# Two of the head's seven transfers moved from the SyncE queue to ScalarE

## The chip, the cores and the metric

The kernel runs on one core of a Trainium2 chip. Times are microseconds of device time. "The time" of a kernel is the median of several executions; the profile and its trace are of one execution.

## The reference

One decoder layer, batch 1, 256 tokens, width 1024, float32. What is computed, cut to its core:

```
h = rms_norm(x, pre_mix_g);  u = h @ w_in                 # 1024 -> 2560 columns
y = concat(conformer_conv(u_conf), short_conv(u_sc), moba_attention(u_att), rglru(u_lru)) @ w_out
x = x + rms_norm(y, post_mix_g)
m = square(relu(rms_norm(x, pre_mlp_g) @ mlp_w1)) @ mlp_w2   # 1024 -> 4096 -> 1024
x = x + rms_norm(m, post_mlp_g)
```

## The kernel before

Activations are held transposed (128 rows of the width, 256 tokens); weights come from HBM as tiles of 128 x 2048 (1 MB). Most products are done in three passes over split numbers: ScalarE rounds a weight tile to a high part (`split_hi`, tiles `hi`), VectorE subtracts to get the low part (`split_lo`, tiles `lo`), and TensorE multiplies high by high, high by low and low by high.

The order of the work is written out by hand: each engine runs its instructions in the order of the text (the class `InOrder`, line 50). Waits between engines are semaphores that the framework places. It tells transfers apart by eight semaphores that are used in turn, so a transfer that comes ninth waits, before it is issued, for the one eight places ahead of it to land.

The start of the kernel, which the change touches, is the *head*: one DRAM tensor that holds the parameters, the transposed input in eight blocks `x0` to `x7` and eight blocks `w0` to `w7` (128 x 256 each) of the first columns of `w_in`. It is loaded into the tile `hd` by seven transfers on the SyncE queue (SP), in the order of `HEAD` (line 45):

```
HEAD = (("x0", "w0"), ("x1", "w1"), ("x2", "x3", "w2"), ("x4", "x5", "w3"), ("x6", "x7", "w4"), ("w5", "w6"), ("w7",))
```

The third to the fifth are 384 KB each, the sixth 256 KB, the seventh 128 KB. Behind them SP issues the first weight tiles (`load(1, 2)`, `load(2, 2)`, each in two halves, and `load(3)`, then `load(4)`), into tiles `raw_in`.

On these blocks the engines work as they come. VectorE scales each x block by its gain (`hf(k)`, tile `hF`), makes `ab` for a small parameter chain behind `hf(2)`, and adds up squares (`add`, tile `sq`). ScalarE loads the Exp table, then does `square(0)`, `h_hi(0)` (rounds to `hT`), `e` (an exponential of `ab`), `square(2)`, `square(4)`, `h_hi(2)`, `square(6)`, a table load for Sqrt, `h_hi(4)`, `h_hi(6)` and the first quarters of `split_hi(1)`. `square(k)` reads the blocks x_k and x_k+1. TensorE multiplies in float32, without splitting (`native(k)`, needs `hF` of block k and the block w_k): k = 0 to 6, then the sum of squares `pss`, then k = 7. From `pss` ScalarE and VectorE make `rstd`; TensorE spreads it as a row (`pR`), ScalarE copies that to `R1` (printed as `R`), and VectorE multiplies projections by it (`cg`, in `conf_gate` and `conf_val`). Behind that the projections of the four mixers follow, then the output projection and the MLP.

GpSimd, meanwhile, fills constants: `warm` for twelve TensorE warm-up products, `ident` (a 128 x 128 identity, a memset and an `affine_select`) and, after it has copied the parameters to `prm`, padding, `identb` (the identity in bfloat16, lines 278 and 279), `bones`, `dist` and others; later a chain of tiny operations that begins with a product of `sr` and `e`. `identb` is first used by `att_scores`.

Of the kernel before, what the change touches and what calls it, by code (L numbers as in the profile page):

```python
# [18 lines left out]
BF16 = mybir.dt.bfloat16  # L19
AF = mybir.ActivationFunctionType  # L20
# [4 lines left out]
P = 128  # L25
S = 256
# [16 lines left out]
PCOLS = C_MLP + KT  # L43

HEAD = (("x0", "w0"), ("x1", "w1"), ("x2", "x3", "w2"), ("x4", "x5", "w3"), ("x6", "x7", "w4"), ("w5", "w6"), ("w7",))
HOFF = {b: PCOLS + i * S for i, b in enumerate(sum(HEAD, ()))}
HCOLS = PCOLS + 2 * KT * S

# [17 lines left out]
def hybrid_layer(ctx, tc, x, head, win, wout, w1, w2, gates, rows, out):  # L66
    nc = tc.nc
    V, A, G, T, Q = (InOrder(tc, e) for e in (nc.vector, nc.scalar, nc.gpsimd, nc.tensor, nc.sync))

    cst = ctx.enter_context(tc.tile_pool(name="cst", bufs=1))  # L70
# [68 lines left out]
    hd = big.tile([P, HCOLS], F32, tag="yy", name="hd")  # L139
    xs = [cst.tile([P, D], F32, name=f"x{t}") for t in range(2)]  # L140
    gw = wk.tile([P, 4, P], F32, name="gw")
    c = 0
    for blocks in HEAD:
        n = HOFF[blocks[-1]] + S
        Q.dma_start(hd[:, c:n], head[:, c:n])
        c = n

    def hb(b):
        return hd[:, HOFF[b]:HOFF[b] + S]

    def xpair(k):
        a, b = HOFF[f"x{k}"], HOFF[f"x{k + 1}"] - HOFF[f"x{k}"]
        return hd[:, a:a + 2 * b].rearrange("p (k c) -> p k c", c=b)[:, :, :S]
# [13 lines left out]
    def pc(t, c, n=1):  # L167
# [8 lines left out]
    ident = cst.tile([P, P], F32, name="ident")  # L176
    G.memset(ident, 1.0)
    G.affine_select(out=ident, in_=ident, pattern=[[-1, P]], compare_op=ALU.is_equal, fill=0.0, base=0,
                    channel_multiplier=1)

# [22 lines left out]
    sr = wk.tile([P, 2], F32, name="sr")  # L206
    s2 = wk.tile([P, 2], F32, name="s2")
    q = wk.tile([P, 2], F32, name="q_")
    A.preload_act_table(AF.Exp)

    def hf(k):
        V.tensor_scalar(hF[:, k, :], hb(f"x{k}"), hd[:, C_PRE + k:C_PRE + k + 1], None, op0=ALU.mult)
# [62 lines left out]
    G.memset(xpad[:, :, :LK - 1], 0.0)  # L275
    cpad = wk.tile([P, 2, SK - 1 + S], F32, name="cpad")
    G.memset(cpad[:, :, :SK - 1], 0.0)
    identb = cst.tile([P, P], BF16, name="identb")
    G.tensor_copy(identb, ident)
    bones = cst.tile([P, P], F32, name="bones")  # L280
    G.memset(bones, 0.0)
    G.memset(bones[0:64, 0:64], 1.0 / 64)
# [962 lines left out]
```

## Time and profile before

| | us |
|---|---|
| median of 3 runs (lowest, highest) | 277.46 (276.95, 277.49) |
| the profiled execution, its own time | 277.3 |
| its span in the trace | 275.6 |
| TensorE busy (matmul) | 266.6, 97% |
| VectorE busy | 257.7, 93% |
| ScalarE busy | 187.9, 68% |
| GpSimd busy | 22.0, 8% |

The span runs from the first to the last instruction of the trace; the profiled execution's own time is 1.7 us longer. Busy shares are means over stages; which engine sets the time in a stage is read from the chain of work that ended last and from the waits. A timeline row gives start, duration, engine (PE is TensorE, PEld its weight loads, DVE VectorE, ACT ScalarE, POOL GpSimd, SPq SyncE's queue), operation, tiles, count, and in brackets the idle time before it with what ended it. All instructions show the one line L60, that of a helper, so the names of tiles tell them apart.

### The profile page before, as it was taken

To read this page: it belongs to the slowest core of one execution; us is meant where nothing else is said; L and a number is where in the kernel's file an instruction comes from. 1 tells how busy PE (TensorE), PEld (TensorE's weight loads), DVE (VectorE), ACT (ScalarE), POOL (GpSimd) and SP (SyncE) were. 2 spreads that over 40 slices of the span, in tenths; PEclk is the share of its full clock that TensorE was granted. 3 is DMA by queue.
4 is the path that set the end of the run, shared out by engine and by line. 5 is a ranking of instruction groups with operands and counts; after the bars stand their busy time and mean duration, and the time that the engine had idled before them with its cause. 6 is when DMAs were issued, how large, how long until landed. Compare 5 with 4: busy or idle time off the path is not lost.

```text
span 275.6 us, 4693 instructions
## 1 busy us (share of the span) xinstructions
PE 266.6 (97%) x1893; PEld 245.2 (89%) x1893; DVE 257.7 (93%) x350; ACT 187.9 (68%) x229; POOL 22.0 (8%) x53
## 2 busy tenths in 40 slices
PE   6999999999999999999999999999999999999991
PEld 4898997999987799899999999999999999999880
DVE  1989999999989999999999999999999999999874
ACT  3895669694557869868468777676885684777341
POOL 4388600000000000000000000000000000000000
PEclk9999999999999999999999999999999999999998
DMA  7998645938502825575375383473562653740004
GB/s 221 396 408 315 233 152 164 373 151 272 182 7 69 312 96 193 194 284 199 115 297 174 133 306 118 190 292 95 225 240 94 277 201 127 283 155 0 0 2 152
DMA packets 9237, 53.04 MB, mean 192 GB/s; under 512 B 1024, under 2 KB 1536, under 8 KB 3712
## 3 DMA queue, kind: packets, MB, share of 16 engines
q1 hardware_dynamic: 9216, 52.75, 51.7%
q8 instruction: 15, 0.25, 0.3%
q14 instruction: 6, 0.05, 0.0%
HBM read 51.70 MB, written 1.05 MB: 191 GB/s over the span
## 4 chain that ended last, share of the span: by engine, by line
PE 91%; DVE 3%; ACT 2%; DMA 2%; issue 1%; SPq 0%; DVEq 0%; ACTq 0%
PE pm L60 30%; PE m_acc L60 17%; PE pu L60 17%; PE acc L60 8%; PE m_sm L60 7%; PE m_mm L60 3%; PE pz L60 2%; DMA hd<-in_head_dram 2%; PE c L60 2%; DVE lo_in L60 1%; PE psc L60 1%; PE po L60 1%; ACT hi_in L60 1%; PE pg L60 1%; DVE u L60 1%
## 5 line engine op out<-in xcount | busy, mean ns | idle before, releaser
L60 DVE TENSOR_TENSOR lo_w<-raw_w,hi_w 128x2048 fp32r<-128x2048 f32 (+3 forms) x38 | 66.9, 1767 | 0.0
L60 ACT ACTIVATE hi_w<-raw_w 128x2048 fp32r<-128x2048 f32 (+2 forms) x35 | 54.5, 1600 | 1.3 <-issue 1.3
L60 ACT ACTIVATE th<-trs 128x2048 fp32r<-128x2048 f32 x13 | 24.9, 1916 | 13.0 <-DVE trs L60 13.0
L60 PE MATMUL pm<-h2T,hi_w 128*128 128x256 f32 x240 | 32.4, 278 | 0.0
L60 PE MATMUL pm<-h2T,lo_w 128*128 128x256 f32 x240 | 32.1, 276 | 0.0
L60 PE MATMUL pm<-h2L,hi_w 128*128 128x256 f32 x240 | 32.1, 276 | 0.0
L60 PEld LDWEIGHTS pm<-h2T,hi_w 128*128 128x128 f32 x240 | 29.9, 188 | 0.1
L60 DVE TENSOR_TENSOR tl<-trs,th 128x2048 fp32r<-128x2048 f32 x13 | 29.7, 2286 | 0.0
L60 PEld LDWEIGHTS pm<-h2T,lo_w 128*128 128x128 f32 x240 | 29.5, 188 | 0.0
L60 PEld LDWEIGHTS pm<-h2L,hi_w 128*128 128x128 f32 x240 | 29.5, 188 | 0.0
L60 DVE SCALAR_TENSOR_TENSOR cacc<-zpad,prm,cacc 128x256 f32<-128x256 f32 x60 | 25.4, 484 | 0.1
L60 ACT ACTIVATE mh<-mf 128x896 fp32r<-128x896 f32 (+2 forms) x16 | 14.1, 881 | 15.2 <-DVE mf L60 15.2
L60 PE MATMUL acc<-hi_out,yy 128*128 128x512 f32 x64 | 21.4, 402 | 0.0
L60 DVE TENSOR_TENSOR lo_in<-raw_in,hi_in 128x2048 fp32r<-128x2048 f32 (+1 forms) x11 | 20.9, 1900 | 0.2
L60 ACT ACTIVATE mr<-pm 128x512 f32<-128x512 f32 x15 | 8.9, 593 | 15.9 <-PE pm L60 15.9
L60 DVE TENSOR_TENSOR trs<-raw_w,trs 128x512 f32<-128x512 f32 x26 | 18.0, 692 | 0.9
L60 PE MATMUL pu<-hT,hi_in 128*128 128x256 f32 x128 | 17.9, 282 | 0.6 <-DVE cg L60 0.6
L60 PE MATMUL m_acc<-hi_w,ml 128*128 128x512 f32 (+1 forms) x57 | 17.9, 389 | 0.0
L60 PE MATMUL m_acc<-hi_w,mh 128*128 128x512 f32 (+1 forms) x57 | 17.7, 385 | 0.0
L60 PE MATMUL m_acc<-lo_w,mh 128*128 128x512 f32 (+1 forms) x57 | 17.7, 385 | 0.0
L60 PE MATMUL pu<-hT,lo_in 128*128 128x256 f32 x128 | 17.4, 278 | 0.1
L60 ACT ACTIVATE hi_in<-raw_in 128x2048 fp32r<-128x2048 f32 (+2 forms) x12 | 17.4, 1479 | 0.0
(235 smaller groups left out, 567.0 us busy)
## 6 DMA issues: line engine op xcount, KB each, us to landing
raw_w<-in_w_dram SPq DMA_DIRECT2D x32, 1024.0 KB, 4.8
raw_in<-in_win_dram SPq DMA_DIRECT2D x7, 1024.0 KB, 5.0
raw_out<-in_wout_dram SPq DMA_DIRECT2D x4, 1024.0 KB, 5.1
raw_in<-in_win_dram SPq DMA_DIRECT2D x4, 512.0 KB, 8.2
hd<-in_head_dram SPq DMA_DIRECT2D x3, 384.0 KB, 5.5
x<-in_x_dram SPq DMA_DIRECT2D x2, 512.0 KB, 6.3
grow<-in_rows_dram SPq DMA_DIRECT2D x2, 512.0 KB, 6.4
hd<-in_head_dram SPq DMA_DIRECT2D x2, 256.0 KB, 4.7
```

The lines of the kernel that those rows point to most:

```text
L60: ins = f(*args, **kwargs)
```

## The change

The transfers that end in the blocks `w3` (the fourth: x4, x5, w3) and `w6` (the sixth: w5, w6) are no longer issued by SP. ScalarE issues them, one after the other. Ahead of them on ScalarE stand the load of the Exp table, which was ScalarE's first instruction already and is only moved up in the text, and the cast of the identity to `identb`, which GpSimd did before. The cast waits for GpSimd's `ident`; the transfers themselves wait for no data.

```diff
+HEAD_A = ("w3", "w6")
@@
     for blocks in HEAD:
         n = HOFF[blocks[-1]] + S
-        Q.dma_start(hd[:, c:n], head[:, c:n])
+        if blocks[-1] not in HEAD_A:
+            Q.dma_start(hd[:, c:n], head[:, c:n])
         c = n
@@ (behind the affine_select of ident)
+    A.preload_act_table(AF.Exp)
+    identb = cst.tile([P, P], BF16, name="identb")
+    A.activation(identb, ident, AF.Copy)
+    for blocks in HEAD:
+        if blocks[-1] in HEAD_A:
+            A.dma_start(hd[:, HOFF[blocks[0]]:HOFF[blocks[-1]] + S], head[:, HOFF[blocks[0]]:HOFF[blocks[-1]] + S])
@@
-    A.preload_act_table(AF.Exp)
@@
-    identb = cst.tile([P, P], BF16, name="identb")
-    G.tensor_copy(identb, ident)
```

## Rows read from the trace of the kernel before

**Rows 1.** Chain of work that ended last, 0 to 30 us: start, us, what

```profile
1.71 4.80 DMA hd<-in_head_dram
...
6.94 4.66 PE pu L60 x20
...
14.09 0.39 ACT R L60
...
25.04 5.04 PE pu L60 x42
```

**Rows 2.** Busy time in stretches: stretch and length; per engine busy us (instructions); PEclk, DMA share, GB/s

```profile
25.00:260.00 235.00, 234.91 (x1693) 217.79 (x1694) 230.37 (x297) 165.01 (x192) 6.73 (x9) 1.00 0.50 186
13.00:25.00 12.00, 11.33 (x98) 10.93 (x96) 10.95 (x15) 9.92 (x12) 10.55 (x19) 1.00 0.94 369
```

**Rows 3.** Timeline of SP's queue: third to sixth head transfer, weights, eleventh issue

```profile
1.71 0.42 SPq L60 DMA_DIRECT2D hd<-in_head_dram  x1
2.17 0.43 SPq L60 DMA_DIRECT2D hd<-in_head_dram  x1
2.65 0.43 SPq L60 DMA_DIRECT2D hd<-in_head_dram  x1
3.12 0.44 SPq L60 DMA_DIRECT2D hd<-in_head_dram  x1
4.08 12.96 SPq L60 DMA_DIRECT2D raw_in<-in_win_dram  x7
6.52 0.33 SPq L60 DMA_DIRECT2D raw_in<-in_win_dram  x1
```

**Rows 4.** DMA issues, third to sixth head transfer: KB each, us from issue to landing

```profile
hd<-in_head_dram SPq DMA_DIRECT2D x1, 384.0 KB, 4.8
...
hd<-in_head_dram SPq DMA_DIRECT2D x1, 384.0 KB, 5.5
...
hd<-in_head_dram SPq DMA_DIRECT2D x1, 384.0 KB, 6.0
...
hd<-in_head_dram SPq DMA_DIRECT2D x1, 256.0 KB, 6.2
```

**Rows 5.** Busy time in stretches of the head (PE, PEld, DVE, ACT, POOL, as rows 2)

```profile
1.50:2.00 0.50, 0.50 (x5) 0.31 (x4) 0.00 (x0) 0.50 (x1) 0.22 (x1) 1.00 0.53 69
...
0.80:3.80 3.00, 2.64 (x12) 1.64 (x12) 0.00 (x0) 1.28 (x1) 0.85 (x6) 1.00 0.62 196
3.50:4.00 0.50, 0.40 (x2) 0.00 (x0) 0.17 (x1) 0.00 (x0) 0.14 (x1) 1.00 1.07 418
4.50:6.50 2.00, 1.83 (x8) 1.27 (x8) 0.44 (x2) 1.16 (x2) 1.60 (x10) 1.00 0.96 257
...
7.00:13.00 6.00, 6.00 (x31) 5.16 (x32) 5.35 (x15) 5.97 (x11) 1.42 (x4) 1.00 1.03 391
```

**Rows 6.** Timeline of ScalarE in the head

```profile
0.79 1.28 ACT L60 ACT_TABLE_LOAD   x1 [0.79 <-PEq L1237]
4.54 0.63 ACT L60 ACTIVATE sq<-hd 128x512 f32<-128x512 f32 x1 [2.46 <-DMA hd<-in_head_dram]
...
6.99 0.20 ACT L60 ACTIVATE e<-ab 128x2 f32<-128x2 f32 x1 [1.29 <-DVE ab L60]
...
8.75 0.61 ACT L60 ACTIVATE sq<-hd 128x512 f32<-128x512 f32 x1
```

**Rows 7.** Timeline of all engines, 0 to 18 us

```profile
4.24 0.29 POOL L60 CAST identb<-ident 128x128 bf16<-128x128 f32 x1
...
7.70 0.35 DVE L60 TENSOR_SCALAR hF<-hd 128x256 f32<-128x256 f32 x1 [0.48 <-DMA hd<-in_head_dram]
...
8.74 2.46 PEld L60 LDWEIGHTS pu<-hF,hd 128*128 128x128 f32 x12 [0.21 <-DVE sq L60]
...
11.34 0.49 POOL L60 TENSOR_TENSOR sr<-sr,e 128x2 f32<-128x2 f32 x1 [4.83 <-ACT hT L60]
```

**Rows 8.** Waits of SP's own queue, 0 to 20 us: us in total, times, longest

```profile
SPq L60 <- DMA hd<-in_head_dram: 2.4, 4, 0.8
```

## The prediction

> **What bounds the kernel now.** I read the chain of work that ended last first, because it says which stage a saving must come from. It starts with the third transfer of the head (issued at 1.71 us, on the chain for 4.80 us), goes through 20 native matmuls (6.94 to 11.60), then ScalarE's copy of the row of factors (14.09) and reaches the long stretch of TensorE work at 25.04 [rows 1]. Behind 25 us TensorE is simply full: 234.91 of 235 us up to 260 [rows 2]. So an edit of the head can move the end only by moving that 25.04; in between (13 to 25 us) TensorE is busy 11.33 of 12 us [rows 2], and the little slack there sits in a chain from ScalarE to VectorE that moves as a whole. The profiled execution is 277.3 us with a span of 275.6 us, so 1.7 us lie outside the span and I leave them alone; the median of the three runs, 277.46, lies 0.16 above it.
>
> Next the transfers. The head's seven transfers are handed in by SP about 0.46 us apart (1.71, 2.17, 2.65, 3.12 for the third to the sixth) but land 4.8, 5.5, 6.0 and 6.2 us after their issue, that is at 6.5, 7.7, 8.65 and 9.3 [rows 3, 4]. The time from issue to landing grows from transfer to transfer: they are not waiting to be issued, they are waiting for each other. The stretches say the same. From 3.5 us on the 16 DMA engines are busy for their whole time and move 418 GB/s, from 7 to 13 us 391 GB/s; only from 4.5 to 6.5 us do they move less, 257 GB/s, and there too they are busy (0.96) [rows 5].
>
> Last the engines behind them. ScalarE does a table load from 0.79 to 2.07 and is then idle until 4.54; from 6.99, when the third transfer has landed and VectorE has made `ab`, it works without a hole to 13 us (5.97 of 6.00 us) [rows 5, 6]. That is what matters: in ScalarE's chain only the third transfer is waited for. The fourth and the fifth arrive just in time for an engine that is already loaded.
>
> **The change, part by part.** Five head transfers stay on SP (first, second, third, fifth, seventh), two go to ScalarE (fourth 384 KB, sixth 256 KB), behind the cast of the identity; the cast leaves GpSimd.
>
> The cast. On GpSimd it takes 0.29 us at 4.24, and GpSimd later idles 4.83 us ahead of the product at 11.34 [rows 7]: removing it there is worth 0. On ScalarE this trace has no cast of 128x128; I bound it by GpSimd's 0.29 us for the same cast [rows 7] and by ScalarE's own 0.63 us for 128x512 [rows 6], and take 0.3, since it has a quarter of those columns. It stands behind the table load, which ends at 2.07, and needs the identity, which GpSimd makes ahead of its work on the head. Then two issues at SP's price, 0.42 to 0.44 us each [rows 3]; ScalarE's issuing is not in this trace, so from 0 to twice that. ScalarE is through at 2.07 + 0.3 + 0.9 = 3.3 us (at worst 2.07 + 0.63 + 1.8 = 4.5), and its first work on the head starts at 4.54 [rows 6]. Cost 0; the cover is that idle stretch, and without it the price would be these 1.2 us. Queued behind them on ScalarE is the first `square`, which waits for the second transfer anyway.
>
> SP's queue. The fifth transfer moves up from 2.65 to 2.17, the seventh to 2.65, and the first weight loads from 4.08 to about 3.1 [rows 3]. What that is worth: the DMA engines are not out of work from 3.5 us on [rows 5], so an earlier place in a queue brings no byte earlier, unless another transfer gives way. The weights win nothing either: the list of waits up to 25 us has no engine that waits for `raw_in`. Worth 0. The Trainium skill says this as a rule (DMA: Bandwidth & Descriptors, section "Issuing engines are not separate DMA queues"): issuing from several engines saves only the sequencer's time, usually small against the transfer. The trace agrees: 0.44 us of issue against 6.2 us to the landing. By a sum that credited issue time instead, 0.9 us would be saved.
>
> The order of arrival. Here is the cost. From 0.8 to 3.8 us the engines move 196 GB/s, 588 kB [rows 5], which is just the first and the second transfer (by the code 618 and 512 columns of 128 x 4 bytes, 579 kB); so the third begins to move at about 3.8 us in the mean. In before everything stands in one queue, and the fourth cannot pass the third. In the change the fourth is handed in between 2.07 and 2.7 us, in another queue. The first transfer, issued at 0.8, moves its first bytes between 1.5 and 2.0 us [rows 5], about 1 us after its issue, so the fourth is ready at 3.1 to 3.7 us, when the third has hardly begun. The engines are full, so each byte of the fourth moved before the third is complete is a byte by which the third is late. The whole fourth is 393 kB; at 418 to 391 GB/s that is 0.94 to 1.01 us. The sixth follows it in ScalarE's queue at once, 262 kB, 0.63 to 0.67 us. No row of before shows two queues of loads side by side, so the delay of the third is bounded by 0 (strictly by time of issue) and by 0.98 + 0.65 = 1.63 us (both of ScalarE's transfers ahead of it). If both queues are served alike, the fourth is through when the third is (same size), and if that starts while the second still moves, the fourth ends early and part of the sixth gets in too. I take the fourth and half of the sixth: 0.98 + 0.32 = 1.3 us, so the third lands at 7.8 us. The Trainium skill describes that service in the same page, section "Queues, rings and completion order": each DMA engine takes turns between the queues that have work. That no run here shows; by it alone the third would be 1.0 to 1.6 us late.
>
> What follows from that. VectorE's `hF` for x2 and `ab`, then ScalarE's `e` at 6.99, all wait for the third, and move to 8.3. Behind `e` ScalarE's chain has no hole, so it is 1.3 us late as a whole. The fourth is then there before it is wanted: VectorE's wait of 0.48 us at 7.70 and TensorE's 0.21 us at 8.74 [rows 7] vanish, but they are not what ends last. The fifth lands behind the sixth, at 8.65 + 0.65 = 9.3 us; `square` on x6, now at 8.75 [rows 6], is due at 10.05, so that hides. The delay therefore goes to the copy at 14.09, to 25.04 and to the end.
>
> Sum: 277.3 + 1.3 + 0 (cast) + 0 (issues) + 0 (SP) = 278.6 us against the profiled execution, 278.76 against the median; I say 278.7. With a delay between 0.65 us (what the sixth alone is worth) and 1.63 us the forecast's own range is 278.1 to 279.1.
>
> **The rivals.** (a) Served in order of issue. Two queues make no difference if the engines take the work as it was handed in; the fourth, handed in at 2.1 to 2.7, then stands beside the fifth, where it stood. For: nothing in the trace speaks against it. Against: the two wait in different queues and something must choose. Gain: TensorE's 0.21 us at most, since ScalarE has no hole to give; 277.1 to 277.5 us.
>
> (b) Faster: the slow spell is cured. From 4.5 to 6.5 us the engines move 257 GB/s instead of 418, so 514 kB take 2.0 us that would take 1.23 [rows 5]. If the engines are held up there because one queue leaves them waiting, a second queue fills the gaps and the third lands up to 0.77 us earlier, with all of the chain: 277.46 - 0.77 = 276.7 us. This decides if the rate in that stretch comes near 400 and the third is not passed. Against: the engines count as busy there (0.96) [rows 5], so the packets themselves are long.
>
> (c) The issues wait. SP itself does not run free: it waits four times, 2.4 us in all, for head transfers to land; its eleventh issue goes at 6.52, when the third has landed [rows 3, 8]. If ScalarE's transfers are counted as they stand in the text, behind ten of SP's, the fourth is the eleventh, leaves at 6.5 and, at the third's 4.8 us, lands at 11.3 instead of 7.7: 3.6 us late for `square` on x4, about 281 us. Against: SP hands in its eighth transfer only at 4.08 [rows 3], long after ScalarE is ready, so by time both stand among the first eight.
>
> **How the numbers follow.** Forecast 0.70, (a) 0.12, (b) 0.12, (c) 0.06. Predicted 278.7 us. The range runs from 277.1, the lower end of (a), to 279.4, the forecast's upper end with 0.3 for a fifth transfer that is late as well; outside lie (b) and (c), 0.18. A measurement of this kernel tells 0.2%, 0.55 us, from no change: faster (under 276.9) 0.12, that is (b); within, (a) and 0.03 of the forecast for a delay under its range, 0.15; slower, the rest of the forecast and (c), 0.73.
>
> **What would show it.** Right: the third transfer lands at 7.5 to 8.1 us instead of 6.5; the fourth lands with it or before; ScalarE's `e` is at 8 or later; TensorE's gap near 25 us sits 1 to 1.6 us later; behind it nothing changes. ScalarE's two issues lie between 2.1 and 3.4 us. Wrong: the third lands at 6.5 as now (a), or before with 400 GB/s from 4.5 to 6.5 us (b), or ScalarE's issues stand behind a wait for a landing (c). I am also wrong if the delay shrinks between 8 and 25 us, which needs slack that I did not see.

## The result, and the profile after

| | before | after |
|---|---|---|
| median, us (lowest, highest), 11 runs each | 277.15 (276.64, 277.74) | 279.72 (278.96, 282.08) |
| ratio, 95% interval | | 1.009 (1.007 to 1.0109) |
| the profiled execution, its own time | 277.3 | 279.05 |
| its span in the trace | 275.6 | 277.3 |

The change makes the kernel slower, by 2.57 us on the medians. A second comparison (e7_after, below) gives 279.34 against 277.42, 1.92 us, ratio 1.0061 (1.0047 to 1.0075). The two profiled executions differ by 1.75 us, and these the traces can account for.

The chain of work that ended last, of after, 0 to 30 us (start, us, what), against [rows 1]:

```profile
1.69 6.16 DMA hd<-in_head_dram
...
11.25 1.97 PE pu L62 x8
...
13.56 1.91 PE pu L62 x12
15.72 0.38 ACT R L62
...
26.67 3.35 PE pu L62 x27
```

The third transfer takes 6.16 us instead of 4.80, and the copy `R` is at 15.72 instead of 14.09. The long stretch of TensorE's work begins at 26.67 instead of 25.04: 1.63 of the 1.75 us are lost before that point. Its beginning follows the row `pu x12` by 13.11 us here (26.67 - 13.56), and by 13.1 to 13.3 us in every kernel of this study, and from that row to the end of the span it is 263.6 to 264.1 us in all of them. So the start of `pu x12` (13.56 here, 11.94 in before) will stand for a kernel's loss in the head.

ScalarE's queue, VectorE and TensorE in the timeline of after, against [rows 3, 6, 7]:

```profile
1.75 0.38 ACTq L62 DMA_DIRECT2D hd<-in_head_dram  x1
2.08 0.31 ACT L62 ACTIVATE identb<-ident 128x128 bf16<-128x128 f32 x1
...
4.45 0.34 ACTq L62 DMA_DIRECT2D hd<-in_head_dram  x1
...
4.83 0.63 ACT L62 ACTIVATE sq<-hd 128x512 f32<-128x512 f32 x1 [2.44 <-DMA hd<-in_head_dram]
...
7.88 0.35 DVE L62 TENSOR_SCALAR hF<-hd 128x256 f32<-128x256 f32 x1 [2.94 <-DMA hd<-in_head_dram]
...
8.29 4.93 PE L62 MATMUL pu<-hF,hd 128*128 128x256 f32 x20 [1.38 <-DVE hF L62]
...
8.34 0.20 ACT L62 ACTIVATE e<-ab 128x2 f32<-128x2 f32 x1 [2.35 <-DVE ab L62]
```

Two things differ from what the prediction assumed. The fourth transfer is handed in at 1.75 us, 0.06 us behind the third and ahead of the cast, while the table load (0.79 to 2.07, as in [rows 6]) still runs. The sixth is handed in only at 4.45 us, just when the second transfer has landed (4.43): in the compiled program each transfer, whichever engine issues it, takes the next of eight completion semaphores. By the semaphore numbers in the trace the fourth is the eighth in that order, and the sixth the tenth: it gets the one of the second transfer, and its issue waits until that is given back.

The landings in after, third, fourth and sixth transfer (KB, us from issue to landing), against [rows 4]:

```profile
hd<-in_head_dram SPq DMA_DIRECT2D x1, 384.0 KB, 6.2
...
hd<-in_head_dram ACTq DMA_DIRECT2D x1, 384.0 KB, 6.3
...
hd<-in_head_dram ACTq DMA_DIRECT2D x1, 256.0 KB, 6.7
```

To the hundredth, by the trace's semaphore records, the third is there at 7.85 us instead of 6.50, the fourth at 8.03 instead of 7.67, the sixth at 11.12 instead of 9.35. The sum of the profiled loss closes with two terms. The 20 native matmuls begin at 8.29 instead of 6.94, 1.35 us later, behind the third. And they take 4.93 instead of 4.66 us, 0.27 us more: the last 8, which need the sixth, begin at 11.25, 0.13 us behind its landing, as in e6_late6 and e7_after (0.14 and 0.13). The chain above names VectorE there, whose last `hF` ends at 11.18, because of two waits it takes the one that ended last; but the first of these matmuls needs `hF` of x5, done at 10.05. The two terms together are 1.62 of the 1.63 us.

Busy time in stretches of after (columns as in [rows 2]), against [rows 5, 2]:

```profile
4.50:6.50 2.00, 2.00 (x7) 1.72 (x8) 0.44 (x2) 1.15 (x2) 1.44 (x8) 1.00 0.99 373
6.50:8.50 2.00, 0.62 (x3) 0.22 (x3) 0.62 (x4) 0.17 (x2) 0.00 (x0) 1.00 0.99 332
7.00:13.00 6.00, 4.60 (x20) 3.79 (x21) 4.86 (x15) 4.63 (x9) 0.49 (x1) 1.00 1.01 378
```

From 4.5 to 6.5 us the DMA engines move 373 GB/s where they moved 257, and still the third is late. ScalarE is busy for 4.63 us between 7 and 13 us instead of 5.97, and from 6.5 to 8.5 us all engines stand almost still.

What the rate doesn't show, the shares do. Each head transfer is split into sixteen shares, and in the trace's records its completion semaphore is raised sixteen times, once as each share arrives; the last one is the landing. The shares of the third transfer, with the sixth's landing, the marker, and the time at which the trace's records of TensorE's granted clock begin (of which the last section tells), in the trace of every kernel (us):

```
kernel            third's shares    the other    sixth    pu x12   clock
                  together, by      shares at    lands    at       recorded from
before            15, 5.43          6.50          9.35    11.94    4.18
e1_before         14, 5.43          6.41, 6.43    9.63    12.18    6.59
e4_cast           15, 5.39          6.24          9.30    11.87    5.40
e6_late6          15, 5.41          6.15         11.07    13.51    6.89
e8_fourth_later   15, 5.44          6.95          9.35    12.80    7.18
e11_both_later    13, 5.42          6.07, 6.60,   9.95    13.15    4.58
                                    7.79
e3_sixth          14, 5.90          6.87, 7.96    8.17    13.31    4.10
after             15, 6.16          7.85         11.12    13.56    5.59
e7_after          15, 6.24          8.12         11.46    13.90    5.78
e10_nowait2       14, 6.13          7.67, 7.85   10.46    13.57    6.02
e2_fourth         16, 6.26                        8.22    13.07    8.51
e5_nowait         16, 6.12                        8.25    12.39    7.19
e9_second         16, 5.59                        9.24    13.21    8.15
```

In before the last share of the third comes 1.07 us behind the other fifteen: that one share is the wait at the head of the chain [rows 1]. In after the fifteen come 0.73 us later than in before, and the last one 1.69 us behind them.

### The profile page after: what moved, and what is told of

Same layout as the page of the kernel before. It is cut to its first block, busy times and chain, and to the rows that moved or that the text cites. A ratio compares the mean times of both kernels' runs of the same rounds, so it can differ in the third digit from the quotient of the medians.

```text
span 277.3 us, 4690 instructions
## 1 busy us (share of the span) xinstructions
PE 267.7 (97%) x1893; PEld 246.2 (89%) x1893; DVE 257.6 (93%) x350; ACT 188.0 (68%) x230; POOL 21.5 (8%) x52
## 3 DMA queue, kind: packets, MB, share of 16 engines
HBM read 51.70 MB, written 1.05 MB: 190 GB/s over the span
## 4 chain that ended last, share of the span: by engine, by line
PE 89%; DVE 4%; DMA 2%; ACT 2%; issue 1%; SPq 0%; DVEq 0%; ACTq 0%
PE pm L62 30%; PE m_acc L62 17%; PE pu L62 15%; PE acc L62 8%; PE m_sm L62 7%; PE m_mm L62 3%; DMA hd<-in_head_dram 2%; PE pz L62 2%; PE c L62 2%; DVE lo_in L62 1%; PE psc L62 1%; PE po L62 1%; ACT hi_in L62 1%; PE pg L62 1%; DVE u L62 1%
## 5 line engine op out<-in xcount | busy, mean ns | idle before, releaser
L62 PE MATMUL pu<-hL,hi_in 128*128 128x256 f32 x128 | 17.5, 279 | 0.0
```

Source lines behind the costliest of these rows:

```text
L62: ins = f(*args, **kwargs)
```

## The experiments

Except where an edit says otherwise, each kernel has the cast and the table load as in the change, and only the set of transfers that ScalarE issues differs.

**The kernel before, again** (no edit).

> The kernel before once more, as a second trace and for the granted clock of each of its executions. All theories: third head transfer lands near 6.5 us, ScalarE's e starts near 7.0, 277.2 us. Theory 'order of arrival' (T1): the slow spell of the DMA engines between 4.5 and 6.5 us (257 GB/s) is there again or not, it is not what the change is about. Theory 'clock' (T3: the part of the loss that the profiled execution doesn't show is TensorE's granted clock falling in a longer hole of the head): every execution of this kernel has a clock of 0.996 or more.

Measured: 277.52 us against 277.62, ratio 0.9993 (0.9984 to 1.0003). The third lands at 6.4 us and `pu x12` is at 12.18. From 4.5 to 6.5 us the engines moved 221 GB/s, so the slow spell of [rows 5] is no accident of one trace. What theory 3 expected did not come: the mean granted clock of the twelve executions runs from 0.993 to 0.998, not from 0.996 up.

**The changed kernel, again** (no edit to it).

> The changed kernel again, for a second trace and a paired time. If its loss is a matter of order, the third transfer lands at 7.5 to 8.0 us, ScalarE's second issue goes out at about 4.4 us, the sixth transfer lands near 11 us, and the median is 2.0 to 2.6 us above the kernel before. If the landing of the third is a matter of chance (one DMA engine that straggles in some executions), it may land near 6.2 us here, with the sixth still near 11 us and the native product of x5 still waiting for it.

Measured: 279.34 us against 277.42, ratio 1.0061 (1.0047 to 1.0075). Chain of e7_after, 0 to 30 us:

```profile
4.54 6.92 DMA hd<-in_head_dram
11.59 1.97 PE pu L62 x8
13.90 1.91 PE pu L62 x12
```

The third landed at 8.1 us, the sixth was again handed in with the second's landing (4.54) and was there at 11.46; here the chain itself goes through it. Both are as in after, and a little later; the median is 1.92 us above the kernel before, just under the 2.0 to 2.6 expected.

**The cast alone.**

```diff
-HEAD_A = ("w3", "w6")
+HEAD_A = ()
```

> Only the cast and the table load stand as in the change (the cast on ScalarE ahead of its first square, the table load asked for earlier in the program, GpSimd's cast gone); all seven transfers stay on SyncE's queue, and no weight tile is written first. Theory 1 (all of the change's loss is in the transfers): the third lands near 6.5 us, e starts near 7.0 and the median is within 0.2 us of the kernel before. Theory 2 (the earlier cast itself costs time, which would be in every kernel of this study but the one before): the median is 0.5 to 1.2 us above the kernel before.

Measured: 277.69 us against 277.56, ratio 1.0009 (0.999 to 1.0028). Chain of e4_cast, 0 to 30 us:

```profile
4.30 7.22 PE pu L62 x28
11.87 1.89 PE pu L62 x12
...
24.96 5.04 PE pu L62 x42
```

The head ends 0.07 us earlier than in before. Theory 1 holds: the cast and the earlier table load cost nothing that can be measured, so the whole loss is in the two transfers.

**The sixth alone, with its wait.**

```diff
-HEAD_A = ("w3", "w6")
+HEAD_A = ("w6",)
```

> Only the sixth transfer (w5, w6) is issued by ScalarE; the other six stay on SyncE's queue, and the first weight tile is loaded as before. ScalarE's issue is expected to wait for the landing of a transfer of the head and to be handed in after 3.5 us instead of 2.9. Theory 1 (in the changed kernel the time is lost because the sixth transfer is handed in late and the native product of x5 waits for it): the third transfer lands near 6.5 us as in the kernel before, the sixth lands between 9.5 and 11 us, the matmuls of w5 and w6 are late by what it lands later than 9.6, and the median is 0.5 to 1.5 us above the kernel before. Theory 2 (the time is lost because a second queue beside the third transfer holds that one up): nothing moves beside the third here, so e starts near 7.0 us and the median is within 0.3 us of the kernel before.

Measured: 279.32 us against 277.42, ratio 1.0056 (1.0042 to 1.0071): as slow as the changed kernel beside it (279.34). Timeline of e6_late6:

```profile
3.81 0.38 ACTq L62 DMA_DIRECT2D hd<-in_head_dram  x1
...
6.18 0.35 DVE L62 TENSOR_SCALAR hF<-hd 128x256 f32<-128x256 f32 x1 [1.22 <-DMA hd<-in_head_dram]
...
6.63 0.20 ACT L62 ACTIVATE e<-ab 128x2 f32<-128x2 f32 x1 [1.01 <-DVE ab L62]
...
11.21 1.97 PE L62 MATMUL pu<-hF,hd 128*128 128x256 f32 x8 [1.05 <-DMA hd<-in_head_dram]
```

ScalarE's issue goes out at 3.81 us, with the first transfer's landing, and the sixth lands 7.26 us later. The third is on time (6.15 us) and `e` is even 0.36 us earlier than in before, and yet TensorE stands still for 1.05 us until the sixth is there at 11.07. Theory 1 holds, and costs more than the 1.5 us that it allowed. The late sixth by itself is enough for the whole loss.

**The sixth alone, at once.** So that its issue needs no landing, ScalarE writes one column of the first weight tile ahead of that tile's load, which overwrites it; the load then stands behind ScalarE's issue in the order of the semaphores. The kernels e2, e5, e8, e10 and e11 do the same. No kernel has that write alone; it takes 0.19 to 0.20 us between 2.3 and 2.9 us, where ScalarE is idle otherwise.

```diff
+HEAD_A = ("w6",)
@@
-    load(1, 2)
-    load(2, 2)
-    load(3)
@@ (behind ScalarE's issues)
+    w_, d_ = new_raw(1)
+    A.activation(w_[:, :1], ident[:, :1], AF.Copy)
+    for i in range(2):
+        Q.dma_start(w_[:, part(i, 2)], d_[:, part(i, 2)])
+    load(2, 2)
+    load(3)
```

> Only the sixth transfer (256 KB) on ScalarE behind the cast, again without a wait for a landing (the same one-column write). T1: it is handed in at about 1.75 us, beside the third, and moves beside it: third late by 262 kB at 400 GB/s, 0.65 us, lands at 7.1 to 7.2; the sixth lands before 8; 277.7 to 278.0 us. T2: third at 6.5, 277.2 us or a little less.

Measured: 278.82 us against 277.62, ratio 1.005 (1.0031 to 1.007). Chain of e3_sixth:

```profile
1.71 6.25 DMA hd<-in_head_dram
...
8.39 4.58 PE pu L62 x20
13.31 1.91 PE pu L62 x12
```

This is the other half of the loss by itself. The sixth, handed in at 1.75 us, is there at 8.17, before it is needed; the third, beside it, lands at 7.96 instead of 6.50, and the 20 matmuls run behind it without a hole (4.58 us) but begin 1.45 us late. By bytes 262 kB should have cost some 0.65 us: theory 1 had the direction, and missed the landing (7.1 to 7.2) and the time (277.7 to 278.0).

**The fourth alone, at once.**

```diff
+HEAD_A = ("w3",)
```

> Only the fourth transfer (384 KB) on ScalarE behind the cast; a one-column write of ScalarE into the first weight tile keeps SP's weight loads behind it in the count of transfers, so that ScalarE's issue waits for no landing. T1 (third is late by what of ScalarE's queue moves beside it, and the sixth's wait for a landing is a second, smaller loss): third lands at 7.5 to 7.9 us, e at 8.0 to 8.4, the sixth on SP lands by 9.6 and TensorE has no hole before native 5; 278.2 to 278.6 us. T2 (the late sixth is the loss, two queues cost nothing by themselves): third at 6.5, 277.2 us. T3: as T1 in the profile, but with single executions 1 to 3 us longer at a clock under 0.995.

Measured: 278.15 us against 277.62, ratio 1.0029 (1.0011 to 1.0046), single runs from 277.43 to 279.99. In the profiled execution (278.54) all sixteen shares of the third came together and it landed at 6.26, earlier than in before, not at 7.5 to 7.9 as theory 1 had it, and still `pu x12` was at 13.07. There the matmuls themselves were slow: see the last section. So this trace does not show what the fourth costs the third; theory 2, no cost, does not hold either, since the median lies 0.53 us above before. Nor does theory 3: the executions of 279.24 to 279.99 us have a clock of 0.997 to 0.998.

**Both at once, without the wait**, two kernels with the same text.

```diff
 HEAD_A = ("w3", "w6")
```

> The changed kernel with both transfers on ScalarE, but without the sixth's wait for the landing of the second (the same one-column write). T1: sixth issued at about 2.2 us and landed by 9.6, TensorE's hole of 0.48 us before native 5 gone; third at 7.8 to 8.4, since part of the sixth now moves beside it too; 278.5 to 279.2 us, a few tenths under the changed kernel. T2: the whole loss is gone, 277.2 us. T3: executions scatter as in the changed kernel (279 to 282) with clocks down to 0.987.

> Both transfers on ScalarE, handed in at 1.75 and 2.2 us with no wait for a landing (the first weight tile is written in one column first, which its load overwrites), once more, for a second trace. Its execution shown so far had the third land at 6.15 us, with no DMA engine behind the others, and was quicker than most of its runs. Theory 1 (a DMA engine that is behind the others in most executions takes packets of both queues in turn, and so holds up the third when the fourth moves beside it): here the third lands at 7.3 to 8.0 us, e starts near 8.2, TensorE's gap near 25 us starts at 26.0 or later, and the sixth lands by 9 us. Theory 2 (the third is always early in this kernel and the loss lies behind it): the third lands by 6.4 us again and the time is lost in the matmuls of the fourth to seventh transfer.

Measured: 278.71 us against 277.62, ratio 1.0045 (1.0029 to 1.0062), and 279.19 against 277.56, ratio 1.0054 (1.0037 to 1.0071). Landings of the third and the fourth, first in e5_nowait, then in e10_nowait2 (KB, us from issue to landing):

```profile
hd<-in_head_dram SPq DMA_DIRECT2D x1, 384.0 KB, 4.4
hd<-in_head_dram ACTq DMA_DIRECT2D x1, 384.0 KB, 4.9
```

```profile
hd<-in_head_dram SPq DMA_DIRECT2D x1, 384.0 KB, 6.2
hd<-in_head_dram ACTq DMA_DIRECT2D x1, 384.0 KB, 6.8
```

One text, handed in at the same times, and the third lands at 6.12 in one execution and at 7.85 in the other. In the first no share is behind the others, in the second two are. So theory 1 of the first expectation missed the third (7.8 to 8.4) in its trace and had the sixth (8.25) and the median right, and theory 1 of the second holds for the third. It was wrong on the sixth: handed in at 2.17 us it landed at 10.46, fourteen of its shares came by 8.51 and the last two at 9.54 and 10.46, and the fifth in SP's queue was held up with it (10.26). Chain of e10_nowait2:

```profile
8.28 1.99 PE pu L62 x8
10.40 2.83 PE pu L62 x12
13.57 1.91 PE pu L62 x12
```

With the sixth's wait gone, TensorE waits for the fifth instead, and `pu x12` is where it is in after. On the medians the wait's removal brings 0.3 to 1.5 us (1.63 and 1.1 us above before, against 1.92 and 2.57), and the intervals overlap in part: it helps, at most, a part of the way.

**The fourth alone, later.** An operation that reads the cast's result stands ahead of the issue.

```diff
+HEAD_A = ("w3",)
+    A.activation(w_[:, :1], identb[:, :1], AF.Copy)
@@ (then the issue)
```

> Only the fourth transfer (x4, x5, w3) is issued by ScalarE, and behind an operation that reads the cast's result, so it is handed in at about 2.5 us instead of 1.75, when the third (handed in at 1.7) has begun and the fifth (2.2) is in its queue. The first weight tile has one column written first, which its load overwrites. Theory 1 (transfers of two queues move roughly in the order in which they are handed in): the third is ahead of it and lands at 5.5 to 6.6 us, the fourth moves beside the fifth and lands at 8 to 9 us, and the median is 0 to 0.8 us above the kernel before. Theory 2 (two queues take turns whenever both hold something): the fourth moves beside the third from its start, the third lands at 7.3 us or later, e starts at 7.8 or later, and the median is 1 us or more above.

Measured: 278.61 us against 277.42, ratio 1.0038 (1.0023 to 1.0054). The issue went out at 2.44 us, fifteen shares of the third came by 5.44 as in before, and it landed at 6.95; the fourth landed at 8.63 and TensorE had waited for it (chain: the transfer from 2.44 for 6.19 us, then matmuls at 8.77), `pu x12` at 12.80. Neither theory fits whole: the third lies between their landings, and the time, 1.19 us above before, is theory 2's by way of the fourth, which is late in its turn (8.63 against 7.67).

**Both later.**

```diff
 HEAD_A = ("w3", "w6")
+    A.activation(w_[:, :1], identb[:, :1], AF.Copy)
@@ (then the two issues)
```

> Both transfers on ScalarE, behind an operation that reads the cast's result and with no wait for a landing: handed in at about 2.45 and 2.85 us, when the third (1.7) is ahead of them. The first weight tile is written in one column first, which its load overwrites. Theory 1 (a transfer moves in the order of its handing in, over both queues): the third lands at 6.2 to 7.0 us, the fourth at 8.3 to 8.9, the sixth at 9 to 10, and the median is 0.8 to 1.3 us above the kernel before, as with the fourth alone (278.6 there), so 0.5 us or more below the changed kernel. Theory 2 (two queues take turns whenever both hold something): the third lands at 7.3 or later and the median is 1.3 us or more above the kernel before.

Measured: 278.69 us against 277.56, ratio 1.0037 (1.0023 to 1.005). Chain of e11_both_later:

```profile
1.69 6.10 DMA hd<-in_head_dram
...
8.23 4.58 PE pu L62 x20
13.15 1.89 PE pu L62 x12
```

The median is where theory 1 put it, for a reason that is not theory 1's. Handed in 0.74 us behind the third, the fourth left thirteen shares of it alone (5.42 us, as in before), but the other three came at 6.07, 6.60 and 7.79, the last 2.37 us behind the thirteen, with two transfers in ScalarE's queue by then. The sixth, handed in at 2.85, landed at 9.95 and was on time: with the wait gone and the fifth in time too (9.54), the third's delay alone is left, and costs 13.15 - 11.94 = 1.21 us in the trace and 1.13 us on the medians.

**The second alone,** as ScalarE's first instruction, so that SP hands in each later transfer some 0.5 us earlier.

```diff
+HEAD_A = ("w1",)
@@ (the issue stands ahead of the table load)
```

> Only the second transfer (x1, w1) is issued by ScalarE, as its first instruction, ahead of the table load; so SyncE hands in each later transfer some 0.5 us earlier, the third at 1.2 us. The cast runs on ScalarE as in the change. If the issues of the head bind (one queue hands in 256 KB each 0.5 us), the third lands 0.3 to 0.5 us earlier than 6.5, e starts at 6.5 to 6.7 us and the median is 0.2 to 0.5 us below the kernel before. If the bytes bind, or the second and the third then move beside each other, the third lands at 6.5 or later and the median is within 0.3 us of the kernel before or above it.

Measured: 279.75 us against 277.42, ratio 1.0074 (1.0055 to 1.0092). In the profiled execution (278.7, the fastest of its six) the third did land early, at 5.59 us, but the first, which then has the second beside it, landed at 4.53 instead of 3.81. The 28 matmuls follow it without a hole, from 5.05 instead of 4.34 us: 0.71 of the 13.21 - 11.94 = 1.27 us there. The other 0.56 is in the matmuls, whose first ones were slow (last section). Neither branch of the expectation has this; what the other executions lose beyond it no trace shows. No kernel of the study is faster than before.

## Why the prediction was wrong in size and right in direction

**What bounds, right.** The loss is in the head, it passes 25 us unchanged, and the rest of the span is the same: 275.6 - 25.04 = 250.56 us behind the marker in before, 277.3 - 26.67 = 250.63 in after.

**The cast, SP's queue, the issues' own time: right, 0.** e4_cast shows it for the cast; the seventh's earlier issue and the weights' bring nothing that a trace shows, though no kernel has them alone.

**The third transfer, right in its landing, wrong in its terms.** Forecast 7.8 us and `e` at 8.3; measured 7.85 and 8.34. But the sum of bytes, 0.98 for the fourth and 0.32 for half of the sixth, is not what happened, so that the landing agrees is luck. The sixth had no part in it, being handed in at 4.45. Sharing the rate with the fourth cost fifteen of the shares 0.73 us, less than a whole fourth. The other 0.62 us is a last share that falls further behind. One to three shares are behind in ten of the thirteen traces: the last of them comes 0.7 to 1.1 us after the shares that came together where nothing of a second queue moves beside the third (before, e1, e4, e6), and 1.5 to 2.4 us after them where something does (e3, e8, e10, e11, after, e7). In e2 and e5 none is behind, with the fourth beside the third as in after. The reading that fits is one DMA engine that is behind and serves both queues: in after the last share of the fourth comes only 0.18 us behind that of the third, though the other fifteen of the fourth are through by 7.14. In after ScalarE's queue moves 66 packets of 3072 bytes from 5.0 to 6.0 us, and from 6.5 to 7.5 only two in each 0.5 us, as SP's fifth and seventh pass it. e3_sixth (the third at 7.96 with 262 kB beside it) and e11_both_later (7.79 with nothing beside thirteen of the shares) speak against the sum by bytes. That the share belongs to one DMA engine is an inference: the records give the count of shares, not which engine served them, and what holds it up was not found. Nor does one share of 24 KB explain the 257 GB/s of [rows 5], which is low for all engines together; that stays open as well.

**The sixth, the step that failed.** "The sixth follows it in ScalarE's queue at once" was wrong, and with it "The fifth lands behind the sixth": it came at 9.00, the sixth 2.1 us after it. Rival (c) had the mechanism, with a chance of 0.06 and for the wrong transfer: it let the fourth wait and argued that by time both stand among the first eight. The order that counts is that of the compiled program: the fourth is the eighth transfer there, the sixth the tenth. So the sixth was handed in at 4.45 us and landed at 11.12, where the forecast had no term at all. In the profiled execution that term is 0.27 us, because the third's delay covers the rest; alone it is 1.57 us (e6_late6: 13.51 - 11.94). The two losses lie side by side: 1.2 to 1.4 us for the third alone (e11_both_later, e3_sixth), 1.57 for the sixth alone, 1.62 for both. Both must go for the head to be as before; in e11_both_later the sixth's part went and 1.2 us stayed.

**The size.** The profile's 1.75 us against the forecast's 1.3 is 0.27 for the sixth, 0.05 for the third and 0.12 behind the head. The median's 2.57 us is more than any trace of after shows. Its profiled execution was the second fastest of eleven; the one of e7_after, 279.57, has the third at 8.12 and the sixth at 11.46, so `pu x12` is at 13.90, 1.96 us late. How far the last share falls behind differs from one execution to the next, and the range, whose upper end was a sum of bytes with 0.3 us on top, had no room for that. The two longest executions of after, 282.08 and 281.24 us, have the lowest mean granted clock of the eleven, 0.987 and 0.992, against 0.993 to 0.998; but in e2_fourth 279.99 us came at 0.997 and 277.67 at 0.993, and neither of the two has a trace. So what made them long stays open. Nor is it known what the other executions lose beyond the traces: a clock that rises late, as in e2_fourth (last section), would add to them, but no trace of them was kept.

**Rivals (a) and (b).** Something of (a) holds, only that the fourth, handed in at 1.75 instead of 2.1 to 2.7 us, stands beside the third and not the fifth. Its first packet moves at 3.91 us, when the second transfer, handed in at 1.22, is nearly through (last packet at 3.98). The sixth, though its queue was otherwise empty for fifteen shares, moved its first packet at 8.03 us, when fifteen shares of SP's fifth and seventh (handed in before it) were in, and then side by side with the first weight tile; in e6_late6, handed in at 3.81, at 7.61, when the first shares of the seventh arrive (7.50). In e11_both_later the fourth left thirteen of the third's shares alone. In these traces transfers handed in within 0.1 us of each other take turns, later ones mostly come later. The Trainium skill (DMA: Bandwidth & Descriptors, section "Queues, rings and completion order") lets each engine take turns between the queues that hold work for it. For the third and the fourth the trace of after agrees, with 118 packets of 3072 bytes from ScalarE's queue against 131 from SP's from 4 to 6 us. For the sixth, counted from its hand-in, it does not: the first packet came 3.6 us later; whether its work had reached the engines before, the records do not show. Of (b) the cure came, 373 GB/s for 257, and brought nothing, since the bytes that filled the spell were the fourth's and not the third's missing share. There was little to gain: in e1_before and e4_cast the third is not on the chain at all, TensorE's 28 matmuls run without a hole from the first transfer on (4.30 to 11.53 us in e4_cast).

## What to carry to other kernels

A transfer that is moved to another engine's queue takes its place in the order of the program's completion semaphores with it: count which transfer's landing its issue will have to wait for, and price the landing from there, not from when the engine is free. A transfer has landed when its last share has: before crediting or charging bandwidth, see whether all shares come together, and do not put another queue's transfer beside the one that the chain waits for. And where two transfers are made late at once, price each alone and take the larger, then see what each removal would leave.

## What the runs showed of the hardware that was not expected

ScalarE hands in a transfer while its table load runs (1.75 us, load from 0.79 to 2.07) and ahead of an operation that stands before it in the text (the cast, at 2.08): its place in the text does not hold it back. In e8_fourth_later an operation ahead of it that waits for the cast's result did, and it went out at 2.44.

The third transfer's last share comes 0.7 to 2.4 us behind the group in ten of the thirteen traces listed above; in three (e2_fourth, e5_nowait, e9_second) all sixteen come together. In e9_second it is the fourth whose last share is behind: fifteen by 6.86 us, its landing at 7.58.

The first native matmuls run at two rates, and the change from one to the other comes at another time in each execution, in before as well. TensorE's native matmuls between 5 and 5.5 us in the kernel before and in e1_before, and between 5.5 and 6 us in e2_fourth (duration in ns, min/median/max, then first and last start):

```profile
L60 PE MATMUL pu<-hF,hd x4: 379/379/379, 4.7 to 5.3; 128*128 128x256 f32 x4
```

```profile
L60 PE MATMUL pu<-hF,hd x3: 634/634/796, 4.3 to 5.3; 128*128 128x256 f32 x3
```

```profile
L62 PE MATMUL pu<-hF,hd x3: 634/634/634, 5.0 to 5.9; 128*128 128x256 f32 x3
```

Those of 634 ns follow each other by 0.43 us, those of 379 ns by 0.215: a factor of two, as between the clock's two levels, 1.2 and 2.4 GHz. The trace's records of the granted clock agree. They begin, with the full clock, at the times in the last column of the table, and in all thirteen traces every matmul that ends before that time is slow and every one that starts behind it is fast. The 1.00 that the stretches give ahead of it stands for no record. TensorE did the same ahead of the change in all (twelve warm-up matmuls from 1.16 to 3.90, native ones from between 4.25 and 5.05 on); why the clock rose at 4.10 in one execution and at 8.51 in another is not shown.

In before slow matmuls are mostly hidden, because TensorE waits for the third anyway (e1_before: 12.18 against 11.94 with the clock up at 6.59). Where the third comes early, they stand on the chain: in e2_fourth nine matmuls are slow, the 28 took 8.32 us, and the gain of an early third was gone. So in e2_fourth, e5_nowait and e9_second part of the loss in the trace is the late clock of that one execution and not the edit's.
